# Seven-product gate-up units that overlap by one product, T1 in a tile of its own, and other places for the modulation products

## The chip, the cores and the metric

The kernel runs on one core of a Trainium2 chip. The metric is the device time of one execution in microseconds (us); the kernel before took 1917.07 us, the median of 3 runs (1916.01 to 1919.67).

## The reference, cut to what matters

A two-layer encoder trunk on x of 512 tokens by 1024 features in float32, conditioned by one vector c. Each layer has two SwiGLU feed-forward networks (FFNs) with a mixer between them:

```
cond = silu(c);  m = cond @ w_mod[l] + b_mod[l]        # shift, scale and gate of three sublayers, 9 x 1024
x = x + 0.5 * m[0,2] * swiglu(adaln(x, m[0]), w1, w3, w2)     # D_FF = 2752
x = x + m[1,2] * (mixer(adaln(x, m[1]) @ w_in) @ w_out)       # layer 0: windowed attention with a relative
x = x + 0.5 * m[2,2] * swiglu(adaln(x, m[2]), w1, w3, w2)     #   bias, short convolution; layer 1: dense
swiglu(h) = (silu(h @ w1) * (h @ w3)) @ w2                    #   attention, Hyena (a small MLP makes its filter)
adaln(x, m) = rmsnorm(x) * g * (1 + m[1]) + m[0]
```

## The kernel before, in words

Features stand on the partitions: x is 8 tiles of 128 features x 512 tokens. A float32 product is three matmuls: each operand is split into a rounded high part (ScalarE, L203) and the rest as a low part (VectorE, L204), and hi x hi, hi x lo and lo x hi are added up in PSUM. Weights are loaded to a `raw` tile of 512 KB (four of them in turn, on SyncE's DMA queue) and split to `wh` and `wl`.

Each of the four FFNs (layer l, place i = 0 or 2) has 21 gate-up units of 128 features (f = 0 to 20) and one of 64 (f = 21), in three groups: f = 0 to 4 and 21, 5 to 12, and 13 to 20. A group is its units and then a *down projection* (`project`, matmuls L358), which in 8 steps `dt` adds the group's part to x (L362). A *plain* unit is 48 matmuls of 512 columns and a glu (`glu`, L513 to L519). A *seven-product* unit (`up_seven`, L465) is Strassen-like: over blocks of 512 features x 256 tokens it needs seven products instead of eight, A11·B11, A12·B21, S2·T2, S1·T1, S3·T3, A22·T4 and S4·B22, each 12 matmuls of 256 columns (L477). S1 to S4 are sums of weight blocks, made on VectorE (`weight_sums`, L454 to L459) and split; T1 to T4 are sums of token blocks of h, made once for an FFN (`token_sums`, L398: h is computed again by L409 and L412, the sums are L418 to L421). T1 is written over the second half of h, so its split has to wait until the plain units have read that. A unit ends with copies and sums of the products (u1 L486, p + u1 L488, u2 L490, c22 L493, c22 + r L494, r + u2 L497), silu (L498), two multiplications (L499, L500) and a split to `ga`, `gb` or `gc`. PSUM has three banks "A", one "V" and two each of "Q" and "C"; A22·T4 goes to the bank that the copy of c22 empties.

The modulation vector m is computed column by column (`gemv`): a load of 512 KB of w_mod (L240) and one multiply-and-sum on VectorE (L248). These products are spread over the program: `rate` (in `ffn`) says how many go with each step of a group's down projection, by (l, i).

The order on each engine comes from a scheduler that moves instructions between the calls; an engine then works strictly down its list, and waits on semaphores. The relative bias (`rel_bias`, matmul L1099) and the Hyena filter (`hyena_filter`) are called between a group's units and its down projection.

## Time and profile before

| what | value |
|---|---|
| median of 3 runs | 1917.07 us |
| the profiled execution's own time; its span | 1918.76 us; 1917.0 us |
| busy: TensorE, VectorE, ScalarE | 1845.9, 1565.1, 1012.5 us |
| mean granted clock of TensorE | 0.988 of full speed |
| bytes from HBM | 258.88 MB |

The profile is one execution. A busy share is a mean over stages with different limits: of a stage one asks which wait ends last there. "PE" is TensorE's matmuls, "PEld" its weight loads, DVE VectorE, ACT ScalarE. A row `A <- B` means that A waited and B ended the wait. `PEclk` is the granted clock of TensorE as a share of full speed (1.00 is 2.4 GHz, 0.50 is 1.2 GHz).

### The profile page before, as it was taken

What the parts mean: (1) busy time and instruction counts of PE and PEld (TensorE: products, weight loads), DVE (VectorE), ACT (ScalarE), POOL (GpSimd) and SP (SyncE); (2) the same over time, 40 slices, a digit from 0 to 9 for tenths busy, and PEclk for the clock granted to TensorE, in tenths of its full rate; (3) what the DMA queues carried; (4) which work ended last, traced back from release to release, by engine and by line L of the source; (5) the groups of instructions that cost most, each with busy time, mean ns of one, the idle gap of its engine ahead of it and who ended that gap; (6) DMA issues with size and microseconds to landing.
All of it is one profiled execution on the core that took longest, in us unless ns stands there. A gap on an engine that the chain in (4) does not pass through costs nothing.

```text
span 1917.0 us, 30306 instructions
## 1 busy us (share of the span) xinstructions
PE 1845.9 (96%) x11844; PEld 1645.8 (86%) x11844; DVE 1565.1 (82%) x2681; ACT 1012.5 (53%) x1651; POOL 3.6 (0%) x9
## 2 busy tenths in 40 slices
PE   7889999999999999999989999998999999999999
PEld 5659889888888899798988989977887898898997
DVE  8989878878759898888899976877887889686682
ACT  5525435378848345254663533555788366353451
POOL 0000000000000000000000000000000000000000
PEclk9989999999999999999999999998999999999999
DMA  7664643842321644636427362344222322333231
GB/s 273 221 229 167 221 145 102 294 132 94 100 85 64 229 148 152 222 99 220 155 95 242 110 220 66 115 135 148 72 88 99 121 89 75 102 104 117 88 119 59
DMA packets 83658, 269.27 MB, mean 140 GB/s; under 512 B 10024, under 2 KB 13352, under 8 KB 83514
## 3 DMA queue, kind: packets, MB, share of 16 engines
q1 hardware_dynamic: 81898, 263.13, 41.0%
q0 software_dynamic: 1616, 4.20, 0.6%
q8 instruction: 93, 1.52, 0.3%
q14 instruction: 51, 0.42, 0.1%
HBM read 258.88 MB, written 10.50 MB: 141 GB/s over the span
## 4 chain that ended last, share of the span: by engine, by line
PE 73%; DVE 16%; DMA 6%; ACT 3%; issue 1%; SPq 0%; ACTq 0%; DVEq 0%
PE pA L477 29%; PE pC L358 18%; PE pV L477 5%; DVE wl L204 3%; PE pA L358 3%; DMA raw<-w2b 3%; DVE raw L248 2%; PE pC L225 2%; PE pC L226 2%; PE pC L224 2%; ACT wh L203 2%; DMA raw<-w2a 1%; DMA raw<-w_mod 1%; PE pA L789 1%; DVE h L345 1%
## 5 line engine op out<-in xcount | busy, mean ns | idle before, releaser
L203 ACT CAST wh<-raw 128x1024 fp32r<-128x1024 f32 (+2 forms) x393 | 372.8, 951 | 547.4 <-PE pA L477 194.6
L204 DVE TENSOR_TENSOR wl<-raw,wh 128x1024 fp32r<-128x1024 f32 (+2 forms) x393 | 432.1, 1102 | 120.3 <-ACT wh L203 117.1
L477 PE MATMUL pA<-h,wh 128*128 128x256 f32 x1752 | 331.2, 283 | 10.1 <-ACT h L203 9.2
L477 PE MATMUL pA<-e,wh 128*128 128x256 f32 x1752 | 333.4, 288 | 6.8 <-ACT tl L486 3.5
L477 PEld LDWEIGHTS pA<-e,wh 128*128 128x128 f32 x1752 | 271.5, 191 | 22.4 <-ACT tq L493 13.1
L477 PEld LDWEIGHTS pA<-h,wh 128*128 128x128 f32 x1752 | 275.7, 191 | 13.3 <-ACT h L203 9.9
L477 PE MATMUL pA<-e,wl 128*128 128x256 f32 x876 | 246.8, 282 | 0.0
L477 PE MATMUL pA<-h,wl 128*128 128x256 f32 x876 | 244.7, 283 | 1.9 <-DVE wl L204 1.9
L358 PE MATMUL pC<-gb,wh 128*128 128x512 f32 (+1 forms) x800 | 227.3, 368 | 3.6 <-ACT gb L203 1.6
L358 PE MATMUL pC<-ga,wh 128*128 128x512 f32 (+1 forms) x648 | 183.6, 371 | 5.0 <-DVE mod L261 2.6
L248 DVE SCALAR_TENSOR_TENSOR raw<-raw,cond 128x1024 f32<-128x1024 f32 x144 | 174.5, 1221 | 15.8 <-DMA raw<-w_mod 14.8
L358 PEld LDWEIGHTS pC<-gb,wh 128*128 128x128 f32 x800 | 143.9, 189 | 34.8 <-ACT gb L203 3.0
L477 PEld LDWEIGHTS pA<-h,wl 128*128 128x128 f32 x876 | 165.6, 189 | 2.3 <-DVE wl L204 2.3
L477 PEld LDWEIGHTS pA<-e,wl 128*128 128x128 f32 x876 | 167.4, 191 | 0.0
L358 PE MATMUL pC<-gb,wl 128*128 128x512 f32 (+1 forms) x392 | 143.8, 367 | 0.0
L358 PEld LDWEIGHTS pC<-ga,wh 128*128 128x128 f32 x648 | 115.5, 189 | 27.7 <-issue 3.9
L362 DVE SCALAR_TENSOR_TENSOR x<-pC,mod,x 128x512 f32<-128x512 f32 (+1 forms) x108 | 74.2, 687 | 74.7 <-PE pC L358 74.3
L358 PE MATMUL pC<-ga,wl 128*128 128x512 f32 (+1 forms) x300 | 111.6, 372 | 5.2 <-DVE wl L204 5.1
L203 ACT CAST wh<-e 128x1024 fp32r<-128x1024 f32 x73 | 76.8, 1052 | 60.6 <-PE pV L477 26.5
L477 PE MATMUL pV<-h,wh 128*128 128x256 f32 x584 | 107.1, 282 | 0.0
L225 PE MATMUL pA<-h,wh 128*128 128x256 f32 (+1 forms) x301 | 90.7, 310 | 2.1 <-DVE h L345 2.1
L477 PEld LDWEIGHTS pV<-h,wh 128*128 128x128 f32 x584 | 90.3, 190 | 0.0
(309 smaller groups left out, 3608.3 us busy)
## 6 DMA issues: line engine op xcount, KB each, us to landing
raw<-w SPq DMA_DIRECT2D x164, 512.0 KB, 3.5
raw<-w_mod SPq DMA_DIRECT2D x144, 512.0 KB, 4.5
raw<-w2b SPq DMA_DIRECT2D x64, 512.0 KB, 4.1
raw<-w_in SPq DMA_DIRECT2D x36, 512.0 KB, 4.5
raw<-w2a SPq DMA_DIRECT2D x32, 384.0 KB, 3.6
raw<-w_out SPq DMA_DIRECT2D x16, 512.0 KB, 3.4
raw<-w_start SPq DMA_DIRECT2D x8, 512.0 KB, 4.7
xs<-x SPq DMA_DIRECT2D x16, 256.0 KB, 2.0
```

The costliest lines, as they stand in the source:

```text
L203: self.nc.scalar.copy(out=hi, in_=src)
L204: self.nc.vector.tensor_sub(out=lo, in0=src, in1=hi.bitcast(F32))
L224: mm(out, lhsT=wh, rhs=rh, start=start, stop=False)
L225: mm(out, lhsT=wh, rhs=rl, start=False, stop=False)
L226: mm(out, lhsT=wl, rhs=rh, start=False, stop=stop)
L248: nc.vector.scalar_tensor_tensor(out=raw, in0=raw, scalar=1.0, in1=self.cond, op0=ALU.mult, op1=ALU.mult, accum_out=m[:, c : c + 1])
L345: nc.vector.tensor_sub(out=lo[:, c0:c1], in0=hf, in1=hi[:, c0:c1].bitcast(F32))
L358: nc.tensor.matmul(ps, lhsT=lh, rhs=r, start=q == 0, stop=q == len(todo) - 1)
L362: nc.vector.scalar_tensor_tensor(out=x, in0=ps, scalar=gate[dt], in1=x, op0=ALU.mult, op1=ALU.add)
L477: nc.tensor.matmul(out, lhsT=lh, rhs=rr, start=first and n == 0, stop=n == 11, skip_group_check=True)
L789: nc.tensor.transpose(tp[:, c * P : (c + 1) * P], pt[qb][:, o : o + P], self.ident)
```

## The change

`up_seven` of a unit now starts with its own A11·B11, then calls the rest of the unit before it (`finish`: A22·T4, the last product, silu, multiplications, split), and goes on with its own A12, S2, S1 and S3. Signs of the sums change so that the multiplications take a factor of -1 (`scalar_tensor_tensor`). Two weight sums stand ahead of the first split. The last unit of a group is finished in two halves. `token_sums` gets h as hi + lo; T1 stays in an `e3` tile and `first_sum` splits it into h after the plain units; the first seven-product unit of an FFN (`late_t1`) takes the product with T1 last. In the first FFN the units 5 to 7 are plain, and the token sums stand at f = 5. `rate` loses one product a step in the first down projection of the first three FFNs; `in_up` puts one product with each unit of some groups: 24 units in all. The relative bias moves from the first FFN's second to its third group. The three small layers of the Hyena filter (`filter_mlp`) move to the third FFN's second group.

```diff
-    def token_sums(self, key):
-
+    def token_sums(self):
 
         nc = self.nc
         t23, t4 = [], []
+        self.t1 = self.t("e3", (P, 1024))
...
-                a, b = self.ab[key + (kt,)]
-                xr = self.t("tq")
-                for c0, r in zip((0, HALF), self.rs):
-                    nc.vector.tensor_mul(
-                        out=xr[:, c0 : c0 + HALF], in0=self.x[kt][:, c0 : c0 + HALF], in1=r)
+                hi, lo = self.h[kt]
                 hf = self.t("th")
-                nc.scalar.activation(out=hf, in_=xr, func=AF.Identity, scale=a, bias=b)
+                nc.vector.tensor_add(out=hf, in0=hi.bitcast(F32), in1=lo.bitcast(F32))
...
-            s14, s23 = self.t("tq"), self.t("tq")
-            s1, s4, s2, s3 = s14[:, :HALF], s14[:, HALF:], s23[:, :HALF], s23[:, HALF:]
-            nc.vector.tensor_sub(out=s1, in0=b12, in1=b11)
-            nc.vector.tensor_sub(out=s2, in0=b22, in1=s1)
+            s4, s23 = self.t("tq")[:, :HALF], self.t("tq")
+            s1, s2, s3 = self.t1[:, j * HALF : (j + 1) * HALF], s23[:, :HALF], s23[:, HALF:]
+            nc.vector.tensor_sub(out=s1, in0=b11, in1=b12)
+            nc.vector.scalar_tensor_tensor(
+                out=s2, in0=s1, scalar=-1.0, in1=b22, op0=ALU.mult, op1=ALU.subtract)
             nc.vector.tensor_sub(out=s3, in0=b22, in1=b12)
-            nc.vector.tensor_sub(out=s4, in0=b21, in1=s2)
+            nc.vector.scalar_tensor_tensor(
+                out=s4, in0=s2, scalar=-1.0, in1=b21, op0=ALU.mult, op1=ALU.subtract)
...
-            self.split(s1, self.h[j][0][:, HALF:], self.h[j][1][:, HALF:])
...
+    def first_sum(self):
+
+        for j in range(4):
+            self.split(
+                self.t1[:, j * HALF : (j + 1) * HALF], self.h[j][0][:, HALF:], self.h[j][1][:, HALF:])
...
+        nc.vector.tensor_add(out=s[:, :T], in0=raw3[:, :T], in1=raw3[:, T:])
+        nc.vector.tensor_add(out=a21, in0=a21, in1=a11)
         x1 = self.split_new(raw1)
-        nc.vector.tensor_add(out=s[:, :T], in0=a21, in1=a22)
-        nc.vector.tensor_sub(out=s[:, T:], in0=s[:, :T], in1=a11)
+        cut = lambda pair, o: [v[:, o : o + T] for v in pair]
+        w = {"A11": cut(x1, 0), "A12": cut(x1, T)}
+        yield w
+        nc.vector.tensor_add(out=s[:, T:], in0=s[:, :T], in1=a11)
         x3 = self.split_new(s)
-        nc.vector.tensor_sub(out=a21, in0=a11, in1=a21)
         x2 = self.split_new(raw3)
-        nc.vector.tensor_sub(out=a12, in0=a12, in1=s[:, T:])
+        nc.vector.tensor_add(out=a12, in0=a12, in1=s[:, T:])
         x4 = self.split_new(a12)
-        cut = lambda pair, o: [v[:, o : o + T] for v in pair]
-        return {"A11": cut(x1, 0), "A12": cut(x1, T), "S1": cut(x3, 0), "S2": cut(x3, T), "S3": cut(x2, 0),
-                "A22": cut(x2, T), "S4": x4}
-
-    def up_seven(self, src1, src3, gh, gl):
-
-        nc = self.nc
-        w = self.weight_sums(src1, src3)
-        q, p, r = self.ps("A")[:, :HALF], self.ps("V")[:, :HALF], self.ps("A")[:, :HALF]
-
-        def product(out, a, b, first):
-            n = 0
-            for j in range(4):
-                wh, wl = (v[:, j * P : (j + 1) * P] for v in w[a])
-                rh, rl = self.rhs7[b][j]
-                for lh, rr in ((wh, rh), (wh, rl), (wl, rh)):
-                    nc.tensor.matmul(
-                        out, lhsT=lh, rhs=rr, start=first and n == 0, stop=n == 11, skip_group_check=True)
-                    n += 1
-
+        w.update({"S1": cut(x3, 0), "S2": cut(x3, T), "S3": cut(x2, 0), "A22": cut(x2, T), "S4": x4})
...
+    def up_seven(self, src1, src3, gh, gl, before, late_t1=False, halves=False):
...
+        sums = self.weight_sums(src1, src3)
+        w = next(sums)
+        q, p = self.ps("A")[:, :HALF], self.ps("V")[:, :HALF]
...
+        self.product(q, w["A11"], "B11", True)
         nc.scalar.copy(out=u1, in_=q)
-        product(p, "A12", "B21", True)
+        if before:
+            before()
+        next(sums, None)
+        r = self.ps("A")[:, :HALF]
+        self.product(p, w["A12"], "B21", True)
         nc.vector.tensor_add(out=sg[:, :HALF], in0=p, in1=u1)
-        product(q, "S2", "T2", False)
+        self.product(q, w["S2"], "T2", False)
         nc.scalar.copy(out=u2, in_=q)
-        product(r, "S1", "T1", True)
-        product(q, "S3", "T3", False)
+        if late_t1:
+            self.product(r, w["S4"], "B22", True)
+        else:
+            self.product(r, w["S1"], "T1", True)
+        self.product(q, w["S3"], "T3", False)
         nc.scalar.copy(out=c22, in_=q)
-        nc.vector.tensor_add(out=c22, in0=r, in1=c22)
-        product(q, "A22", "T4", False)
-        product(r, "S4", "B22", False)
-        nc.vector.tensor_add(out=sg[:, HALF:], in0=r, in1=u2)
-        nc.scalar.activation(out=sg, in_=sg, func=AF.Silu)
-        nc.vector.tensor_mul(out=sg[:, :HALF], in0=sg[:, :HALF], in1=q)
-        nc.vector.tensor_mul(out=sg[:, HALF:], in0=sg[:, HALF:], in1=c22)
-        self.split(sg, gh, gl)
+        nc.vector.tensor_tensor(out=c22, in0=c22, in1=r, op=ALU.subtract if late_t1 else ALU.add)
+
+        def finish():
+            self.product(q, w["A22"], "T4", False)
+            if late_t1:
+                self.product(r, w["S1"], "T1", False)
+                nc.vector.tensor_add(out=c22, in0=c22, in1=r)
+            else:
+                self.product(r, w["S4"], "B22", False)
+            neg = dict(scalar=-1.0, op0=ALU.mult, op1=ALU.mult)
+            if halves:
+                a, b = sg[:, :HALF], sg[:, HALF:]
+                nc.scalar.activation(out=a, in_=a, func=AF.Silu)
+                nc.vector.scalar_tensor_tensor(out=a, in0=q, in1=a, **neg)
+                self.split(a, gh[:, :HALF], gl[:, :HALF])
+                nc.vector.tensor_add(out=b, in0=r, in1=u2)
+                nc.scalar.activation(out=b, in_=b, func=AF.Silu)
+                nc.vector.scalar_tensor_tensor(out=b, in0=c22, in1=b, **neg)
+                self.split(b, gh[:, HALF:], gl[:, HALF:])
+                return
+            nc.vector.tensor_add(out=sg[:, HALF:], in0=r, in1=u2)
+            nc.scalar.activation(out=sg, in_=sg, func=AF.Silu)
+            nc.vector.scalar_tensor_tensor(out=sg[:, :HALF], in0=q, in1=sg[:, :HALF], **neg)
+            nc.vector.scalar_tensor_tensor(out=sg[:, HALF:], in0=c22, in1=sg[:, HALF:], **neg)
+            self.split(sg, gh, gl)
+
+        return finish
...
-        rate = {(0, 0): (2, 2, 2), (0, 2): (2, 2, 2), (1, 0): (2, 1, 0), (1, 2): (0, 0, 0)}[l, i]
+        rate = {(0, 0): (1, 2, 2), (0, 2): (1, 2, 2), (1, 0): (1, 1, 0), (1, 2): (0, 0, 0)}[l, i]
+        in_up = {(0, 0): (2,), (1, 0): (1, 2)}.get((l, i), ())
...
+            pending = None
             for f in fs:
                 gt[f] = new_g()
+                if g in in_up:
+                    self.gemv(1)
...
-                        self.token_sums((l, i))
-                elif first and g == 0:
+                        self.token_sums()
+                        self.first_sum()
+                elif first and (g == 0 or f < 8):
                     ps = self.up_banks()
                     for s in range(2):
                         w = self.weight(self.up_unit(k, 2 * f + s))
                         for kt in range(KT):
                             self.mm3(ps[s], self.block(w, kt), self.h[kt], kt == 0, kt == KT - 1)
-                        self.gemv(4)
+                        if g == 0:
...
+                            self.gemv(4)
                     self.glu(ps[0], ps[1], P, *gt[f])
-                    self.token_sums((l, i))
+                    if f == 5:
+                        self.token_sums()
+                    if f == 7:
+                        self.first_sum()
                 else:
-                    self.up_seven(self.up_unit(k, 2 * f), self.up_unit(k, 2 * f + 1), *gt[f])
-            if (l, i, g) == (0, 0, 1):
+                    pending = self.up_seven(
+                        self.up_unit(k, 2 * f), self.up_unit(k, 2 * f + 1), *gt[f], pending,
+                        late_t1=f == (8 if first else 2), halves=f == fs[-1])
+            if pending:
+                pending()
+            if (l, i, g) == (0, 0, 2):
                 self.rel_bias()
+            if (l, i, g) == (1, 0, 1):
+                self.filter_mlp()
             if (l, i, g) == (1, 0, 2):
                 self.hyena_filter()
...
-    def hyena_filter(self):
+    def filter_mlp(self):
...
-        w4 = self.t("raw", (P, 1024))[:64]
...
+        self.fsrc = src
+
+    def hyena_filter(self):
+
+        nc, ap = self.nc, self.ap
+        src = self.fsrc
+        w4 = self.t("raw", (P, 1024))[:64]
+        nc.sync.dma_start(out=w4, in_=ap["f_w4"])
```

On TensorE, in the second group of the last FFN: `pA_17379` holds S3·T3 and then A22·T4 of a unit, `pA_17507` A11·B11 of the next unit. Before:

```order
L477 MATMUL pA_17379<-e_2998_16752,wl_17371 128x256
L477 MATMUL pA_17507<-h_16274,wh_17487 128x256
L477 MATMUL pA_17507<-h_16275,wh_17487 128x256
L477 MATMUL pA_17507<-h_16274,wl_17488 128x256
L477 MATMUL pA_17507<-h_16276,wh_17487 128x256
L477 MATMUL pA_17379<-e_2972_16680,wh_17370 128x256
L477 MATMUL pA_17379<-e_2973_16681,wh_17370 128x256
L477 MATMUL pA_17379<-e_2972_16680,wl_17371 128x256
```

After, with `pA_17225` and `pA_17353` in these roles; the first two matmuls of A11·B11 stand ahead of the piece, behind S3·T3:

```order
L476 MATMUL pA_17353<-h_16055,wl_17350 128x256
L476 MATMUL pA_17353<-h_16057,wh_17349 128x256
L476 MATMUL pA_17353<-h_16058,wh_17349 128x256
L476 MATMUL pA_17353<-h_16057,wl_17350 128x256
L476 MATMUL pA_17353<-h_16059,wh_17349 128x256
L476 MATMUL pA_17353<-h_16060,wh_17349 128x256
L476 MATMUL pA_17353<-h_16059,wl_17350 128x256
L476 MATMUL pA_17353<-h_16061,wh_17349 128x256
L476 MATMUL pA_17353<-h_16062,wh_17349 128x256
L476 MATMUL pA_17353<-h_16061,wl_17350 128x256
L476 MATMUL pA_17225<-e_2926_16456,wh_17278 128x256
L476 MATMUL pA_17225<-e_2927_16457,wh_17278 128x256
```

Before, four matmuls of the next unit stood between S3·T3 and A22·T4; now all twelve do.

On VectorE, in the first down projection: L248 is a modulation product, L204 a split of weights, L362 the update of x. Before:

```order
L248 SCALAR_TENSOR_TENSOR raw_930,mod_1_0_864<-raw_930,cond 128x1024
L204 TENSOR_TENSOR wl_935<-raw_933,wh_934 128x768
L248 SCALAR_TENSOR_TENSOR raw_959,mod_1_0_864<-raw_959,cond 128x1024
L362 SCALAR_TENSOR_TENSOR x_68<-pC_908,mod_0_16_676,x_68 128x512
L625 CAST wh_934<-wl_935 64x128
L248 SCALAR_TENSOR_TENSOR raw_962,mod_1_0_864<-raw_962,cond 128x1024
L204 TENSOR_TENSOR wl_967<-raw_965,wh_966 128x768
L362 SCALAR_TENSOR_TENSOR x_69<-pC_940,mod_0_16_676,x_69 128x512
L625 CAST wh_966<-wl_967 64x128
L248 SCALAR_TENSOR_TENSOR raw_991,mod_1_0_864<-raw_991,cond 128x1024
L248 SCALAR_TENSOR_TENSOR raw_994,mod_1_0_864<-raw_994,cond 128x1024
L204 TENSOR_TENSOR wl_999<-raw_997,wh_998 128x768
```

After:

```order
L248 SCALAR_TENSOR_TENSOR raw_850,mod_1_0_764<-raw_850,cond 128x1024
L204 TENSOR_TENSOR wl_855<-raw_853,wh_854 128x768
L248 SCALAR_TENSOR_TENSOR raw_879,mod_1_0_764<-raw_879,cond 128x1024
L362 SCALAR_TENSOR_TENSOR x_67<-pC_773,mod_0_16_676,x_67 128x512
L672 CAST wh_854<-wl_855 64x128
L204 TENSOR_TENSOR wl_884<-raw_882,wh_883 128x768
L248 SCALAR_TENSOR_TENSOR raw_908,mod_1_0_764<-raw_908,cond 128x1024
L672 CAST wh_883<-wl_884 64x128
L204 TENSOR_TENSOR e_204_1050<-tq_1044,e_203_1049 128x512
L362 SCALAR_TENSOR_TENSOR x_68<-pC_802,mod_0_16_676,x_68 128x512
L204 TENSOR_TENSOR wl_913<-raw_911,wh_912 128x768
L248 SCALAR_TENSOR_TENSOR raw_937,mod_1_0_764<-raw_937,cond 128x1024
```

Two modulation products stood between two updates of x, and now one does; a split of a token sum (`e_204`) comes between.

On VectorE, at the start of the second FFN's seven-product units: `wl_6363` (before) and `wl_6149` (after) are the low part of A11 and A12 of the first of them, `e_` splits of token sums, `h_` splits of T1, L514 and L516 (L547, L549) the glu of plain units. Before:

```order
L204 TENSOR_TENSOR wl_6363<-raw_6357,wh_6362 128x1024
L457 TENSOR_TENSOR raw_6486<-raw_6485,raw_6486 128x512
L419 TENSOR_TENSOR tq_6292<-th_6289,tq_6291 128x256
L514 TENSOR_TENSOR tc_6210<-tc_6210,pA_5984 128x512
L420 TENSOR_TENSOR tq_6292<-th_6289,th_6284 128x256
L421 TENSOR_TENSOR tq_6291<-th_6289,tq_6292 128x256
L409 TENSOR_TENSOR tq_6305<-x_5449,rb_5745 128x256
L516 TENSOR_TENSOR ga_6209<-tc_6210,ga_6208 128x512
L204 TENSOR_TENSOR h_5870<-tq_6265,h_5869 128x256
L204 TENSOR_TENSOR e_1158_6298<-tq_6292,e_1157_6297 128x512
L204 TENSOR_TENSOR e_1150_6276<-tq_6291,e_1149_6275 128x256
L204 TENSOR_TENSOR h_5872<-tq_6291,h_5871 128x256
```

After:

```order
L414 SCALAR_TENSOR_TENSOR tq_6120<-e_1110_6062,th_6117 128x256
L204 TENSOR_TENSOR h_5677<-e_1110_6062,h_5676 128x256
L417 SCALAR_TENSOR_TENSOR tq_6119<-tq_6120,th_6117 128x256
L549 TENSOR_TENSOR ga_6023<-tc_6055,ga_6022 64x512
L204 TENSOR_TENSOR e_1138_6126<-tq_6120,e_1137_6125 128x512
L552 CAST ga_6023<-ga_6023 64x512
L204 TENSOR_TENSOR e_1132_6112<-tq_6119,e_1131_6111 128x256
L204 TENSOR_TENSOR h_5679<-e_1110_6062,h_5678 128x256
L204 TENSOR_TENSOR h_5681<-e_1110_6062,h_5680 128x256
L204 TENSOR_TENSOR h_5683<-e_1110_6062,h_5682 128x256
L456 TENSOR_TENSOR e_1143_6143<-raw_6142 128x512
L204 TENSOR_TENSOR wl_6149<-raw_6141,wh_6148 128x1024
```

The first unit's weights stood between the token sums of the first and the second block, and now stand behind all of these and behind the four splits of T1.

## Rows read from the trace of the kernel before

**Rows 1.** The page, busy us by engine (share of the span) x instructions.
```profile
PE 1845.9 (96%) x11844; PEld 1645.8 (86%) x11844; DVE 1565.1 (82%) x2681; ACT 1012.5 (53%) x1651; POOL 3.6 (0%) x9
```

**Rows 2.** Chain of waits, 1684 to 1706 us: start us, us, what x count.
```profile
1684.05 1.41 PE pV L477 x12
1685.46 8.74 PE pA L477 x72
```

**Rows 3.** Waits, weight loads (PEld) and matmuls (PE): us in total, times, longest.
```profile
PEld pA L477 <- ACT tq L493: 13.1, 66, 0.4
...
PE pA L477 <- ACT h L203: 9.2, 3, 3.1
PE pQ L992 <- DVE acc L978: 5.7, 1, 5.7
PE pC L358 <- ACT gc L203: 5.4, 5, 1.8
...
PE pA L477 <- ACT tl L486: 3.5, 2, 2.4
```

**Rows 4.** Windows, one unit: stretch, length, busy (x) by engine, PEclk, DMA share, GB/s.
```profile
1684.11:1694.26 10.15, 10.15 (x86) 9.96 (x85) 9.04 (x14) 5.79 (x10) 0.00 (x0) 1.00 0.31 102
```

**Rows 5.** Timeline, same unit: start, us, instruction, [idle before <-releaser].
```profile
1684.11 1.22 DVE L204 TENSOR_TENSOR wl<-raw,wh 128x1024 fp32r<-128x1024 f32 x1 [0.54 <-ACT wh L203]
...
1689.75 0.37 ACT L493 COPY tq<-pA 128x256 f32<-128x256 f32 x1 [0.48 <-PE pA L477]
```

**Rows 6.** The page, costliest groups: L204 and L248, busy, mean ns.
```profile
L204 DVE TENSOR_TENSOR wl<-raw,wh 128x1024 fp32r<-128x1024 f32 (+2 forms) x393 | 432.1, 1102 | 120.3 <-ACT wh L203 117.1
...
L248 DVE SCALAR_TENSOR_TENSOR raw<-raw,cond 128x1024 f32<-128x1024 f32 x144 | 174.5, 1221 | 15.8 <-DMA raw<-w_mod 14.8
```

**Rows 7.** Lines L362 and L499: count, ns min/median/max.
```profile
L362 DVE SCALAR_TENSOR_TENSOR x<-pA,mod,x x21: 385/484/752, 540.3 to 1561.2; 128x256 f32<-128x256 f32 x14, 128x512 f32<-128x512 f32 x7
...
L499 DVE TENSOR_TENSOR tc<-tc,pA x73: 404/414/423, 152.3 to 1871.7; 128x256 f32<-128x256 f32 x73
```

**Rows 8.** Windows, first down projection.
```profile
82.00:145.00 63.00, 47.12 (x198) 33.60 (x197) 56.99 (x107) 20.27 (x31) 1.24 (x1) 0.89 0.59 198
120.00:136.00 16.00, 13.45 (x54) 9.22 (x52) 13.07 (x24) 3.55 (x4) 0.00 (x0) 1.00 0.84 287
```

**Rows 9.** Chain of waits, first down projection.
```profile
87.74 0.60 DVE gb L516
...
132.17 3.76 PE pC L358 x15
```

**Rows 10.** The page, DMA issues: count, KB each, us to landing.
```profile
raw<-w_mod SPq DMA_DIRECT2D x144, 512.0 KB, 4.5
...
raw<-w2a SPq DMA_DIRECT2D x32, 384.0 KB, 3.6
```

**Rows 11.** Chain of waits, a down projection without stalls.
```profile
675.98 3.93 PE pC L358 x17
```

**Rows 12.** Chain of waits, start of the second FFN.
```profile
603.89 0.60 DVE tc L514
604.48 0.34 DVE tq L420
...
628.50 1.41 PE pV L477 x12
```

**Rows 13.** Timeline of TensorE, start of the second FFN.
```profile
609.11 0.40 PE L477 MATMUL pA<-h,wh 128*128 128x256 f32 x2
...
617.66 0.38 PE L477 MATMUL pA<-h,wh 128*128 128x256 f32 x1 [3.08 <-ACT h L203]
```

**Rows 14.** Windows around three stops of TensorE.
```profile
614.00:628.00 14.00, 9.98 (x55) 8.93 (x55) 12.69 (x24) 7.67 (x12) 0.00 (x0) 0.76 0.29 86
680.00:690.00 10.00, 7.56 (x52) 7.36 (x51) 9.93 (x15) 5.15 (x7) 0.00 (x0) 0.83 0.34 120
1290.00:1308.00 18.00, 11.62 (x57) 9.89 (x57) 13.99 (x26) 9.54 (x17) 0.00 (x0) 0.72 0.09 29
```

More of the change, by code (lines that the diff above doesn't have):

```diff
@@ L391, in project @@
         self.new_h()
-        self.rs = rs
         for c0, r in zip((0, HALF), rs):
@@ L448, in weight_sums @@
         raw1, raw3 = self.t("raw", (P, 1024)), self.t("raw", (P, 1024))
+        s = self.t("e3", (P, 1024))
+        a11, a12, a21 = raw1[:, :T], raw1[:, T:], raw3[:, :T]
         nc.sync.dma_start(out=raw1, in_=src1)
         nc.sync.dma_start(out=raw3, in_=src3)
-        s = self.t("e3", (P, 1024))
-        a11, a12, a21, a22 = raw1[:, :T], raw1[:, T:], raw3[:, :T], raw3[:, T:]
+        nc.vector.tensor_add(out=s[:, :T], in0=raw3[:, :T], in1=raw3[:, T:])
+        nc.vector.tensor_add(out=a21, in0=a21, in1=a11)
@@ new lines, in product @@
+    def product(self, out, w, b, first, last=False):
+        n = 0
+        for j in range(4):
+            wh, wl = (v[:, j * P : (j + 1) * P] for v in w)
+            rh, rl = self.rhs7[b][j]
+            for lh, rr in ((wh, rh), (wh, rl), (wl, rh)):
+                self.nc.tensor.matmul(
+                    out, lhsT=lh, rhs=rr, start=first and n == 0, stop=n == 11, skip_group_check=True)
+                n += 1
+    def up_seven(self, src1, src3, gh, gl, before, late_t1=False, halves=False):
+        nc = self.nc
+        sums = self.weight_sums(src1, src3)
+        w = next(sums)
+        q, p = self.ps("A")[:, :HALF], self.ps("V")[:, :HALF]
@@ L484, in up_seven @@
         sg = self.t("tc")
-        product(q, "A11", "B11", True)
+        self.product(q, w["A11"], "B11", True)
         nc.scalar.copy(out=u1, in_=q)
-        product(p, "A12", "B21", True)
+        if before:
[3 more added lines that the diff above has]
+        self.product(p, w["A12"], "B21", True)
         nc.vector.tensor_add(out=sg[:, :HALF], in0=p, in1=u1)
-        product(q, "S2", "T2", False)
+        self.product(q, w["S2"], "T2", False)
         nc.scalar.copy(out=u2, in_=q)
-        product(r, "S1", "T1", True)
@@ L548, in ffn @@
                             r = self.first_rstd()
-                            self.rs = [r[:, c0 : c0 + HALF] for c0 in (0, HALF)]
                             w = self.weight(self.ap["w13_start"][0])
@@ L918, in fold, with sin_tile @@
         nc.vector.tensor_sub(out=minus, in0=pe, in1=o)
-    def sin_tile(self, p, freq, freqb):
+    def sin_tile(self, p, freq, freqb, tag="tq"):
         nc = self.nc
-        a, k = self.t("tq")[:64], self.t("tq")[:64]
+        a, k = self.t(tag)[:64], self.t("tq")[:64]
         nc.scalar.activation(out=a, in_=p, func=AF.Identity, scale=freq, bias=freqb)
@@ L944, in hyena_filter @@
         nc.sync.dma_start(out=fc[:, :4], in_=ap["f_cols"])
-        nc.sync.dma_start(out=w4, in_=ap["f_w4"])
         for s in range(3):
@@ L951, in hyena_filter @@
             nc.tensor.matmul(p, lhsT=lw[s], rhs=src, start=True, stop=True)
-            src = self.sin_tile(p, fc[:, 3:4], fc[:, 4 + s : 5 + s])
+            src = self.sin_tile(p, fc[:, 3:4], fc[:, 4 + s : 5 + s], "tq" if s < 2 else "rb")
+        self.fsrc = src
[4 more added lines that the diff above has]
+        nc.sync.dma_start(out=w4, in_=ap["f_w4"])
         delta = self.t("rb")
```

## The prediction

> **What bounds the kernel now.** I read the page's busy times first: TensorE is busy for 1845.9 of 1917.0 us, VectorE for 1565.1, ScalarE for 1012.5 [rows 1]. So TensorE bounds the kernel, VectorE is the engine behind it, and a change can only gain by fewer or cheaper matmuls, or by filling the 71 us in which TensorE has no matmul and the stretches in which its clock is low. The chain of waits in a steady stretch of seven-product units shows how one unit costs 10.15 us: 12 matmuls in 1.41 and 72 in 8.74 [rows 2]. At 1.41 / 12 = 0.1175 us each, 84 matmuls would need 9.87 us; 0.28 us a unit is lost. The list of waits says where: the weight loads of L477 wait 66 times for the copy of c22 (L493), 13.1 us in all [rows 3]. In the windows view such a unit holds 9.04 us of VectorE work in 10.15 us, at clock 1.00 [rows 4]; the timeline shows the copy starting 0.48 us late, when the matmuls of S3 end, and VectorE's longest idle time of the unit, 0.54 us [rows 5]. The other losses are local: three waits for the split of T1, 9.2 us; one in the Hyena filter, 5.7 us; five for the last glu before a down projection, 5.4 us; two at the start of a group, 3.5 us [rows 3]. And there is one stretch where TensorE doesn't set the pace at all: from 82 to 145 us, the first down projection, it is busy for 47.12 of 63 us at a mean clock of 0.89 while VectorE is busy for 56.99 [rows 8].
>
> **Seven-product units that overlap.** The first order piece shows that four of the twelve A11 matmuls already stood ahead of A22. Now all twelve do, 1.41 us of cover for a copy whose wait is 0.28, so the wait goes. 73 such units ran before (the count of L499, [rows 7]); 70 remain. Of these, 24 now get a modulation product each (below). Of the other 46, eight are the last of their group, where no A11 follows; that leaves 38 x 0.28 = 10.6 us. TensorE's matmuls in a unit are the same in number.
> VectorE must fit under 9.87 us for that. Its list has the same 14 operations; two multiplications become scalar_tensor_tensor. The nearest rows are 484 ns for that form on a 128x256 PSUM tile against 414 for L499's multiplication [rows 7], so 9.04 + 2 x 0.07 = 9.18 us, 0.69 below the bound. The late idle of 0.54 us still fits (9.72). I take the full 10.6; if the slack were not enough, it would be nothing.
> The 24 units (third group of the first FFN, second and third of the third) are another matter: one modulation product costs 1.22 us on VectorE [rows 6], and 9.18 + 1.22 = 10.40 is above both 9.87 and 10.15. They become bound by VectorE: 24 x 0.25 = 6 us lost. Bounds: 24 x (9.87 - 10.15) = 6.7 us gained, if part of the list slides into idle time at the groups' ends, and with the 0.54 us wait left in, 10.94, 24 x 0.79 = 19 us lost. I take 6 lost.
>
> **The first down projection, fewer modulation products, three plain units.** Before, each of its 8 steps carried two modulation products (second order piece): two loads of 512 KB beside 384 KB of weights [rows 10], 1408 KB at the 287 GB/s of this stretch, which is 4.9 us, with DMA busy at 0.84 [rows 8], and the token sums and the relative bias besides. TensorE's own work for a step is 17 matmuls in 3.93 us [rows 11]. After, a step loads 896 KB, some 3.1 us at that rate, and VectorE has in it at most 1.10 (weights' low half), 1.22 [rows 6] and 0.75 (update, the longest in rows 7), 3.1 us: TensorE becomes the bound at 3.93 us. I let it start where the last gate-up value of the group came ready before, at 87.74 + 0.60 = 88.3 [rows 9], because the modulation products ahead of it in VectorE's order stay. Then 88 + 8 x 3.93 = 119.4 us instead of the 135.9 at which the last step ended (132.17 + 3.76) [rows 9]: 16.5 us gained. Paid back: the units 5 to 7 become plain, 48 matmuls of 512 columns at 3.93 / 17 = 0.231 us = 11.1 us instead of 10.15, 3 us in all. The token sums on VectorE lie beside their matmuls. Net 13.5 us gained. Bounds: 4 (if the loads still set the pace in half of the steps) to 19 (if the step starts 5 us earlier as well).
> The same at the start of the next groups: the first weights of the second FFN's second group come late, behind modulation products of the down projection; the two waits for the copy of u1 are 3.5 us [rows 3], and the clock in the 10 us from 680 on is 0.83 [rows 14], another 1.7. With one product a step instead of two both go: 5 us gained, bounds 0 and 7.
>
> **T1 in a tile of its own.** Three FFNs begin with token sums. Before, TensorE reached the first seven-product unit at 609.11, did 48 matmuls and stopped for 3.08 us at 617.66 for the split of T1 [rows 13]; the clock of 614 to 628 was 0.76 [rows 14]. The A12 product of the next unit began at 628.50 [rows 12]. What stands ahead of the unit's first weights in VectorE's order is what decides, and the third order piece shows that this got longer: wl of the first unit now stands behind all token sums and the four splits of T1. From the glu operation of the second plain unit on (L514 at 603.89 [rows 12], L547 after, itself counted) 25 VectorE instructions stand ahead of it; at 0.34 us from start to start for 256 and 0.60 for 512 columns [rows 12], and some 0.07 more for the scalar_tensor_tensor ones, these are 11.6 us, and wl itself 1.10 [rows 6]: ready at 616.6. So TensorE stands still from 609.1 to about 616.6, then has 96 matmuls (11.3 us), 1 to 1.5 us of waits for the next weights, and a low clock for some of it: 629 to 633 us for what ended at 628.50. The removed wait comes back, somewhat larger, ahead of the first product. I take 2 us lost each, 6 in all; bounds 9 us gained (the waits of rows 3 gone, nothing in their place) and 13 lost.
>
> **Tails and the Hyena filter.** The first step of a down projection waited for the last unit's output in five groups, 5.4 us by the row for gc alone [rows 3]. Now the last unit comes in halves, and 21 matmuls of the projection, 4.9 us, stand ahead of that wait in the last FFN, where 17 stood. Some of the five may be weights that land late instead, so I take 4 gained, bounds 0 and 6. The filter's small layers move to an earlier group; the wait for acc (5.7 us, [rows 3]) and the clock of 0.72 in the 18 us around it [rows 14], 5 us, have other causes beside these layers. I take 5 of 10.7; bounds 0 and 10.
>
> **Sum.** -10.6 + 6 - 13.5 - 5 + 6 - 4 - 5 = -26.1 us. The profiled execution took 1918.8 us, 1.8 beyond its span and 1.7 above the median of the three runs, 1917.1. From the median: 1891 us.
>
> **Rivals.** *VectorE becomes the bound of every seven-product unit (slower).* The margin of 0.69 us is in-order time: the sums of the next unit now stand early in VectorE's list and can wait for their weights while the multiplications behind them are due. For it: 9.18 of 9.87 us, and 82% busy overall [rows 1]. Against it: its longest idle time in a unit is 0.54 us. If all 70 units ran at 10.60 us, the gain of 10.6 would become a loss of 70 x 0.45 = 31.5 in place of the 6: -26.1 + 10.6 - 6 + 31.5 = +10, 1927 us. The break-even is a period of 10.46 us; from about 10.51 the kernel is measurably slower.
> *The clock pays for the longer stops.* TensorE standing still 7.5 us at three FFN starts, and near 88 us, could leave it at 1.2 GHz for longer than the 6 us lost hold: at 617 us 3.08 us of waiting were followed by 14 us at 0.76 [rows 13, 14], so a further 14 x 0.24 = 3.4 us each, 10 in all: 1901 us. For the stop itself the third order piece speaks; against the price, that the granted clock was low there before, too. [...]
> *The first down projection stays bound by loads and VectorE.* With only 4 of its 13.5 us gained: 1900 us. For it: DMA at 0.84 busy. Against: 36% fewer bytes.
> *The T1 and product terms cost nothing.* The two losses of 6 us are absorbed, VectorE's idle times at the ends of groups taking up the one, and the other not arising because the first unit's weights are split sooner than I count: 1879 us.
> *Nothing remains.* The two costs at their bounds (19 and 13 lost) and the first down projection at 4: 1917.1 + (-10.6 + 19 - 4 - 5 + 13 - 4 - 5) = 1920.5 us.
>
> **Chances.** The forecast (1891, its own range 1883 to 1898) 0.47; absorbed losses 0.16; clock 0.13; first down 0.12; nothing remains 0.05; VectorE everywhere 0.07. 0.2% is 3.8 us, about what a measurement of this kernel can tell from no change. Faster by more than that: all of the first four and the lower part of the fifth, 0.90; within it the rest of the fifth and a little of the last, 0.04; slower 0.06. The range 1870 to 1907 leaves out the last two cases and the far ends of the others.
>
> **What will show it.** Right: the wait for c22 gone from the list, units of 84 matmuls each 9.87 us in the last FFN; units of 10.4 us with VectorE without idle time in the third FFN; in the first down projection updates of x 3.9 us apart, the last near 119 us; TensorE idle for 7 us at about the start of the first unit in three FFNs, waiting for wl or h. Wrong: units above 10.15 us where no modulation product runs, or updates in the first down projection still 5 us apart.

## The result, and the profile after

The changed kernel takes 1896.3 us (median of 4 runs, 1892.0 to 1898.7); its ratio to the kernel before is 0.9891, with a 95% interval from 0.9867 to 0.9915. Measured again beside later experiments: 1894.6 us, ratio 0.9877 (0.9857 to 0.9896). That is 21 to 24 us faster; 26 were forecast. The profiled execution took 1898.7 us, with a span of 1896.9. A second one was profiled with the later measurement (span 1892.8); single stages of the two differ by up to 4 us, and where that matters both are given.

Busy times after, which answer to [rows 1]:

```profile
PE 1831.8 (97%) x11736; PEld 1642.3 (87%) x11736; DVE 1547.3 (82%) x2634; ACT 987.9 (52%) x1625; POOL 3.6 (0%) x9
```

TensorE is busy for 14 us less and idle for 6 us less; matmul stalls of some tenths and slow matmuls count as busy here (a unit of 10.15 us was busy for all of it, [rows 4]), and the mean clock is 0.986, where it was 0.988. The waits of weight loads for the copy of c22, which answer to the first line of [rows 3]:

```profile
PEld pA L476 <- ACT tq L507: 3.4, 11, 0.9
```

13.1 us in 66 waits have become 3.4 in 11. The longest waits of matmuls after:

```profile
PE pA L476 <- DVE wl L204: 19.2, 3, 6.9
PE pC L358 <- DVE x L362: 7.4, 3, 4.2
```

The first is new: two waits of 6.9 us and one of 5.3 at the starts of FFNs, in the place of the three for T1's split. The second stands in third down projections, twice in the first FFN (2.2 and 4.2 us) and once in the second. In the last FFN the unit's period can be read on VectorE, from one unit's first multiplication to the next one's:

```profile
1699.07 0.42 DVE L530 SCALAR_TENSOR_TENSOR tc<-pA,tc 128x256 f32<-128x256 f32 x1
...
1708.96 0.42 DVE L530 SCALAR_TENSOR_TENSOR tc<-pA,tc 128x256 f32<-128x256 f32 x1
```

9.89 us, where it was 10.15 [rows 4]. These rows also show the form that I priced 0.07 us above a plain multiplication: 0.42 us, as before.

Windows after, each for a stage with its own story: the first down projection and what follows it ([rows 8] before), the start of the second FFN ([rows 14]), the third down projection of the first FFN, the first mixer, and the end of the third FFN with the Hyena filter:

```profile
82.00:145.00 63.00, 59.98 (x247) 47.94 (x246) 53.38 (x91) 21.05 (x28) 0.00 (x0) 0.95 0.56 183
605.00:620.00 15.00, 8.06 (x46) 7.74 (x45) 14.91 (x27) 7.15 (x12) 0.00 (x0) 0.66 0.08 24
335.00:390.00 55.00, 48.52 (x290) 43.31 (x289) 40.73 (x72) 20.87 (x34) 1.24 (x1) 0.94 0.78 276
390.00:531.00 141.00, 137.55 (x731) 113.34 (x730) 113.08 (x242) 106.73 (x231) 0.00 (x0) 1.00 0.32 105
1254.00:1316.00 62.00, 61.98 (x396) 53.34 (x396) 46.98 (x78) 35.12 (x57) 0.00 (x0) 1.00 0.39 136
```

And the last three stages before:

```profile
348.60:397.30 48.70, 45.87 (x290) 40.55 (x289) 39.95 (x71) 21.06 (x34) 0.00 (x0) 1.00 0.77 262
397.30:534.30 137.00, 136.21 (x731) 112.84 (x729) 113.50 (x243) 109.72 (x234) 0.00 (x0) 1.00 0.34 107
1253.00:1334.00 81.00, 72.94 (x416) 59.89 (x416) 61.12 (x106) 42.38 (x67) 0.00 (x0) 0.94 0.32 111
```

The stage with the filter runs at a clock of 1.00, where it was 0.94. Its two windows do not begin at the same matmul; from the last matmul of the third FFN's units to the last one of the down projection it is 81.7 us before and 66.2 after, so 15.5 us shorter. Before:

```profile
1251.92 0.28 PE L477 MATMUL pA<-h,wl 128*128 128x256 f32 x1
...
1333.64 0.28 PE L358 MATMUL pC<-gc,wl 128*128 128x256 f32 x1
```

After:

```profile
1250.20 0.28 PE L476 MATMUL pA<-h,wl 128*128 128x256 f32 x1
...
1316.37 0.28 PE L358 MATMUL pC<-gc,wl 128*128 128x256 f32 x1
```

The third down projection went from 48.7 to 55 us and the mixer from 137 to 141: there the change lost what nothing in my sum spoke of. The lead over the kernel before, read at the last matmul of some stages, shows how the gain comes about:

| up to the end of | first profile, us ahead | second profile, us ahead |
|---|---|---|
| the units of the first FFN's second group | 14.7 | 16.8 |
| the first FFN's third down projection | 7.1 | 8.2 |
| the second FFN | 3.5 | 7.4 |
| the units of the third FFN's third group | 1.7 | 5.4 |
| the Hyena filter and the down projection beside it | 17.3 | 20.9 |
| the kernel | 20.1 | 24.2 |

The lead of the first FFN is mostly lost again, and the stage with the filter brings the larger part of the net gain. Of the low point, 2 to 4 us are the filter's small layers, which the change has done by then: the second down projection of the third FFN, which now holds them, is that much longer than before.

### The profile page after: what moved, and what is told of

It is laid out like the page before. It is cut to its first block, busy times and chain, and to the rows that moved or that the text cites. A ratio compares the mean times of both kernels' runs of the same rounds, so it can differ in the third digit from the quotient of the medians.

```text
span 1896.9 us, 29947 instructions
## 1 busy us (share of the span) xinstructions
PE 1831.8 (97%) x11736; PEld 1642.3 (87%) x11736; DVE 1547.3 (82%) x2634; ACT 987.9 (52%) x1625; POOL 3.6 (0%) x9
## 4 chain that ended last, share of the span: by engine, by line
PE 79%; DVE 12%; DMA 5%; ACT 2%; issue 1%; SPq 0%; ACTq 0%; DVEq 0%
PE pA L476 26%; PE pC L358 20%; PE pV L476 4%; PE pA L358 4%; DVE wl L204 3%; DMA raw<-w2b 3%; PE pC L225 2%; PE pC L224 2%; PE pC L226 2%; DVE raw L248 2%; PE pA L225 2%; PE pA L226 2%; PE pA L224 2%; DMA raw<-w_mod 1%; ACT wh L203 1%
## 5 line engine op out<-in xcount | busy, mean ns | idle before, releaser
L203 ACT CAST wh<-raw 128x1024 fp32r<-128x1024 f32 (+2 forms) x390 | 371.6, 954 | 484.4 <-PE pA L476 137.1
L204 DVE TENSOR_TENSOR wl<-raw,wh 128x1024 fp32r<-128x1024 f32 (+2 forms) x390 | 429.7, 1104 | 97.1 <-ACT wh L203 92.2
L476 PE MATMUL pA<-e,wh 128*128 128x256 f32 x1680 | 309.2, 282 | 2.6 <-ACT tl L501 2.5
L476 PE MATMUL pA<-h,wh 128*128 128x256 f32 x1680 | 309.1, 282 | 0.4 <-DVE tc L528 0.4
L476 PEld LDWEIGHTS pA<-e,wh 128*128 128x128 f32 x1680 | 257.6, 189 | 7.3 <-ACT tl L501 3.8
L476 PEld LDWEIGHTS pA<-h,wh 128*128 128x128 f32 x1680 | 259.9, 191 | 1.7 <-DVE tc L528 0.6
L476 PE MATMUL pA<-h,wl 128*128 128x256 f32 x840 | 238.2, 284 | 19.2 <-DVE wl L204 19.2
L476 PE MATMUL pA<-e,wl 128*128 128x256 f32 x840 | 234.9, 280 | 0.0
L248 DVE SCALAR_TENSOR_TENSOR raw<-raw,cond 128x1024 f32<-128x1024 f32 x144 | 174.9, 1220 | 17.3 <-DMA raw<-w_mod 16.6
L476 PEld LDWEIGHTS pA<-h,wl 128*128 128x128 f32 x840 | 159.3, 190 | 19.8 <-DVE wl L204 19.8
L476 PEld LDWEIGHTS pA<-e,wl 128*128 128x128 f32 x840 | 158.4, 189 | 0.0
L362 DVE SCALAR_TENSOR_TENSOR x<-pC,mod,x 128x512 f32<-128x512 f32 (+1 forms) x108 | 74.1, 686 | 74.5 <-PE pC L358 74.3
L225 PE MATMUL pA<-h,wh 128*128 128x256 f32 (+1 forms) x333 | 102.9, 316 | 1.2 <-DVE h L345 1.2
L226 PE MATMUL pA<-h,wl 128*128 128x256 f32 (+1 forms) x333 | 102.7, 313 | 0.0
```

What stands on the lines that cost most here:

```text
L203: self.nc.scalar.copy(out=hi, in_=src)
L204: self.nc.vector.tensor_sub(out=lo, in0=src, in1=hi.bitcast(F32))
L225: mm(out, lhsT=wh, rhs=rl, start=False, stop=False)
L226: mm(out, lhsT=wl, rhs=rh, start=False, stop=stop)
L248: nc.vector.scalar_tensor_tensor(out=raw, in0=raw, scalar=1.0, in1=self.cond, op0=ALU.mult, op1=ALU.mult, accum_out=m[:, c : c + 1])
L362: nc.vector.scalar_tensor_tensor(out=x, in0=ps, scalar=gate[dt], in1=x, op0=ALU.mult, op1=ALU.add)
```

## The experiments

All but one start from the changed kernel. A ratio is to the kernel before, timed in the same set of runs.

**The overlap.** The next unit begins only after `finish`:

```
-                        late_t1=..., halves=f == fs[-1])
+                        late_t1=..., halves=f == fs[-1])
+                    pending()
+                    pending = None
```

> Changed kernel, but each seven-product unit is finished before the next begins in program order (the scheduler may still move matmuls). Theory: the overlap of one product is what took away the wait for the copy of c22; without it 38 units cost 0.28 us more, units of 10.15 us in the last FFN instead of 9.87, about 1896 + 10 = 1906 us. Rival: the gain in these units is from the new order of the weight sums, and the scheduler pulls A11 ahead anyway: 1896 to 1899 us and units of 9.9 us.

1901.0 us, ratio 0.9918 (0.9893 to 0.9942), between the theory's 1906 and the rival's 1899. The wait for the copy of c22 is back, and a unit of the last FFN takes 10.16 us again (1676.85 - 1666.69):

```profile
PEld pA L476 <- ACT tq L507: 12.9, 64, 0.8
```

```profile
1666.69 0.42 DVE L530 SCALAR_TENSOR_TENSOR tc<-pA,tc 128x256 f32<-128x256 f32 x1
...
1676.85 0.42 DVE L530 SCALAR_TENSOR_TENSOR tc<-pA,tc 128x256 f32<-128x256 f32 x1
```

So the theory holds in the rows: 9.5 us more of that wait. By the ratios the kernel is 5 to 8 us slower, with intervals that leave room for 10.

**The modulation products where they were before.**

```
-        rate = {(0, 0): (1, 2, 2), (0, 2): (1, 2, 2), (1, 0): (1, 1, 0), ...
-        in_up = {(0, 0): (2,), (1, 0): (1, 2)}.get((l, i), ())
+        rate = {(0, 0): (2, 2, 2), (0, 2): (2, 2, 2), (1, 0): (2, 1, 0), ...
+        in_up = ()
```

> Changed kernel with the modulation products where they were before: two a step in the first down projections of the first three FFNs, none with the units. Theory: the first down projection was bound by the loads of these products, so its steps go back from about 4.3 to about 5 us, 6 to 10 us more there, 5 us more at the start of the second FFN's second group, and 2 to 4 us less in the groups whose units lose their product: 1904 to 1908 us. Rival: what slowed that projection were the token sums and the relative bias, which stay away: its steps stay near 4.3 us and the time at 1893 to 1898 us.

1893.2 us, ratio 0.9884 (0.9853 to 0.9914): the rival's time, though the edit also takes the products out of the units, so that the time alone does not part the two. In the first down projection the updates of x, here the first and the seventh, come as early as in the changed kernel. Changed kernel:

```profile
93.35 0.75 DVE L362 SCALAR_TENSOR_TENSOR x<-pC,mod,x 128x512 f32<-128x512 f32 x1
...
118.93 0.75 DVE L362 SCALAR_TENSOR_TENSOR x<-pC,mod,x 128x512 f32<-128x512 f32 x1
```

With two products a step:

```profile
92.22 0.75 DVE L362 SCALAR_TENSOR_TENSOR x<-pC,mod,x 128x512 f32<-128x512 f32 x1 [0.16 <-PE pC L358]
...
116.24 0.75 DVE L362 SCALAR_TENSOR_TENSOR x<-pC,mod,x 128x512 f32<-128x512 f32 x1
```

**Where the relative bias stands.** In the changed kernel the relative bias's transfer of 2 MB, issued by GpSimd at 337.6 us, runs beside the weight loads of the third down projection. The edit calls it in the loop over units, behind unit 8:

```
+                if (l, i, f) == (0, 0, 8):
+                    self.rel_bias()
...
-            if (l, i, g) == (0, 0, 2):
-                self.rel_bias()
```

> Changed kernel with the relative bias called after the first seven-product unit (f = 8) of the first FFN, so that its transfer of 2 MB runs beside seven-product units. Theory: in the changed kernel this transfer lies in the third down projection of the first FFN, whose loads land later for it (55.2 us instead of 48.7): 6 us less there and perhaps 1 to 3 in the mixer behind it, 1887 to 1890 us. Rival: that projection is slower because of the modulation products' own loads behind units that now also load them: no change, 1894 to 1898 us.

1886.5 us, ratio 0.9842 (0.9819 to 0.9866). GpSimd's issue of the transfer in the changed kernel, and here:

```profile
337.58 1.24 POOL L1158 DMA_DIRECT2D vec<-vec  x1 [337.13 <-DMA vec<-th]
```

```profile
164.69 1.24 POOL L1158 DMA_DIRECT2D vec<-vec  x1 [164.25 <-DMA vec<-th]
```

And the third down projection and the mixer here:

```profile
334.30:386.20 51.90, 47.10 (x290) 42.16 (x289) 40.73 (x72) 20.95 (x34) 0.00 (x0) 0.97 0.75 253
386.20:523.30 137.10, 136.32 (x730) 112.97 (x729) 113.51 (x243) 109.65 (x234) 0.00 (x0) 1.00 0.34 107
```

Some 3 us come back in the projection, and all 4 in the mixer. Before, the transfer was issued at 141 us, among the units. The projection's own weights (`w2b`) land later beside it. Time from issue to landing in us (the last figure), changed kernel from 330 to 392 us, and this one from 326 to 388:

```profile
raw<-w2b SPq DMA_DIRECT2D x5, 512.0 KB, 7.9
```

```profile
raw<-w2b SPq DMA_DIRECT2D x6, 512.0 KB, 4.8
```

The other 3 us of the projection's 6.5 stay when the transfer has gone.

**The filter's layers called where they were.** `filter_mlp()` directly ahead of `hyena_filter()`:

> Changed kernel with the three small layers of the Hyena filter called right before the rest of the filter, as before, in the third FFN's third group. Theory: the stage from that group's down projection to the mixer, 80.7 us before and 62.2 after, is shorter by 18.5 us because these layers no longer stand in one chain with the rest of the filter: 1896 + 15 = 1911 us (14 to 19 more). Rival: the layers' own waits were 3 us and the rest of the 18.5 comes from elsewhere: 1897 to 1901 us.

1909.0 us, ratio 0.9955 (0.9939 to 0.9970): 12 to 15 us slower by the ratios, at the theory's lower end and far from the rival. The stage is as long as before, at as low a clock:

```profile
1240.00:1322.00 82.00, 72.10 (x410) 59.05 (x409) 60.16 (x104) 44.50 (x68) 0.00 (x0) 0.92 0.32 110
```

**What held the first down projection.** First, units 5 to 7 as seven-product units and the token sums behind unit 4, as before:

```
-                elif first and (g == 0 or f < 8):
+                elif first and g == 0:
...
-                    if f == 5:
+                    if f == 4:
                         self.token_sums()
-                    if f == 7:
                         self.first_sum()
...
-                        late_t1=f == (8 if first else 2), ...
+                        late_t1=f == (5 if first else 2), ...
```

> Changed kernel with units 5 to 7 of the first FFN as seven-product units again, and the token sums, the splits of T1 among them, called right behind unit 4, as before. Rates and relative bias stay as changed. Theory: the token sums on VectorE are what held the first down projection back, not the loads (with two products a step it ended as early as with one): its steps go back to 5 us or more, 8 to 12 us lost, 3 us of the plain units gained: 1901 to 1906 us. Rival: the matmul of the relative bias and its load did it, which stay away: the projection keeps its 37 us, and the time is 1892 to 1895 us.

1894.0 us, ratio 0.9875 (0.9858 to 0.9891), which meets the rival's number for another reason: the scheduler had pulled the relative bias forward into this projection.

```profile
PE pQ L1151 <- DMA th<-rel_hot: 8.2, 1, 8.2
```

The second down projection began 12 us late, at 217.3 us, and later stages gave it back, since the transfer no longer met the third: that projection and the mixer took 10 us less. So this run didn't tell the two apart. Two more do, with the product of the relative bias in a bank A, so that it can't move ahead of the units. In the kernel before:

> The kernel before, with one edit: the relative bias called behind unit 8 of the first FFN, its product in one of the banks A so that it stays among the units, and away from the first down projection. Theory: in that projection VectorE's token sums set the pace, and TensorE waiting 5.2 us for the relative bias's table cost next to nothing beside them: 1914 to 1917 us. Rival: TensorE's wait for this table and the low clock behind it were the loss there: 8 to 13 us gained, 1904 to 1909 us.

1917.3 us, ratio 0.9995 (0.9982 to 1.0007): no gain. The wait for the table is gone, and another stands in its place, for weights behind the token sums in VectorE's list:

```profile
PE pC L358 <- DVE wl L204: 11.0, 4, 9.8
```

And in the variant of the changed kernel:

> The kernel with units 5 to 7 of the first FFN as seven-product units and the token sums in the first down projection, now with the relative bias behind unit 8 as well, its product in one of the banks A. Theory: the token sums on VectorE cost the first down projection and the units behind it 8 to 12 us even without the relative bias: against the kernel with the relative bias moved alone (1886.5 us) 1894 to 1898 us, the second down projection of the first FFN starting at 213 to 217 us instead of 205. Rival: only the relative bias slowed that projection: 1882 to 1887 us, that start at 203 to 206 us.

1891.5 us, ratio 0.9861 (0.9844 to 0.9878); the second down projection begins at 209.8 us, between the two theories' figures (before: 220.2; with plain units 204.8). The wait is the same one:

```profile
PE pC L358 <- DVE wl L204: 11.4, 1, 11.4
```

The first projection itself takes 44.8 us from its first to its last matmul, where the kernel with the relative bias moved alone takes 35.8: the token sums in it cost 9 us. To take them out costs the 3.6 us of three plain units, so that the move is worth 5 us of that stretch. The other 10 us of the 15 come with cheaper sums, the overlap, one product a step and the relative bias's absence together, and I didn't part these; by `rates_back` one product a step isn't the main part.

**The halves.** `halves=False`:

> Changed kernel without the two halves in the last unit of a group. Theory: the halves bring nothing where a down projection has modulation products, since one of these stands between the halves on VectorE (at 648 us TensorE waits 2.4 us): 1894 to 1898 us, that wait back at about 1.2 us. Rival: the halves are worth the predicted 4 us: 1899 to 1902 us, waits for gc and gb longer in all groups.

1891.2 us, ratio 0.9866 (0.9849 to 0.9883): no slower than the changed kernel.

**T1's product in third place.** `late_t1=False`:

> Changed kernel in which the first seven-product unit of an FFN takes the product with T1 in third place, as all others do; T1 stays in its own tile. Theory: TensorE's wait at the start of that unit is for the low part of A11's weights behind all token sums on VectorE, 7 us, and the order of its products changes nothing in it: 1895 to 1898 us, the same three waits of about 7 us. Rival: the late product is what keeps a second wait, for T1's split, away: 2 to 3 us more in each of three FFNs, 1902 to 1906 us.

1893.3 us, ratio 0.9874 (0.9856 to 0.9893), with the same three waits, 19.2 us. The order of the products makes no measurable difference there.

**A plain unit for the token sums to stand beside.** On top of the moved relative bias:

```
-                    if not first:
-                        self.token_sums()
-                        self.first_sum()
-                elif first and (g == 0 or f < 8):
+                elif first and (g == 0 or f < 8) or f == 2:
...
-                    if f == 5:
+                    if f == (5 if first else 2):
                         self.token_sums()
-                    if f == 7:
+                    if f == (7 if first else 2):
                         self.first_sum()
...
-                        late_t1=f == (8 if first else 2), ...
+                        late_t1=f == (8 if first else 3), ...
```

> The kernel with the relative bias behind unit 8 (1886.5 us), and unit 2 of the other three FFNs a plain one, so that the token sums stand beside its 48 matmuls and its weights ahead of most of them on VectorE; the first seven-product unit is then unit 3. Theory: the three waits of 7 us for the weights and the low clock behind them, 8 to 10 us each, go, and each plain unit costs 1.2 us more than a seven-product one: 6 to 8 us gained in each, 1863 to 1869 us. Rival: VectorE's list is what bounds the start and has got two more splits: the wait only moves behind the plain unit, 1885 to 1890 us.

1863.4 us, ratio 0.9725 (0.9706 to 0.9743), 22 to 23 us below the kernel with the relative bias moved alone, and 29 to 33 below the changed one. The three waits for `wl` are gone from the list. 50 us at the start of the second FFN, in both from 59 us behind the end of the mixer, changed kernel and this one:

```profile
590.00:640.00 50.00, 43.06 (x323) 41.82 (x322) 47.73 (x88) 29.40 (x51) 0.00 (x0) 0.90 0.21 67
```

```profile
580.00:630.00 50.00, 49.06 (x333) 44.89 (x332) 48.88 (x90) 28.60 (x49) 0.00 (x0) 1.00 0.31 103
```

TensorE has 6 us more matmul time and its clock is 1.00 instead of 0.90; the mean over the kernel is 0.999.

**The same without the halves,** and **the changed kernel again:**

> The kernel with unit 2 plain and the relative bias moved (1863.4 us), without the two halves in the last unit of a group. Theory: the halves bring nothing, the modulation products on VectorE come between them: 1860 to 1865 us. Rival: the halves bring the predicted 4 us: 1866 to 1869 us.

1864.8 us, ratio 0.9723 (0.9703 to 0.9743): the halves bring nothing here either.

> The changed kernel itself, for a closer interval beside the others: every theory expects 1893 to 1898 us.

1894.6 us, as given above.

## Why the prediction was right, and where it wasn't

The direction and the size held: 21 to 24 us where 26 were forecast. But that the sum came out is in good part luck: several terms were off, and two large errors cancelled. Without the filter's move the kernel gains 6 to 12 us (`filter_back`), where the sum without that term was 21; the filter's move brought 7 to 10 us more than forecast, and the relative bias, which the sum left out, cost 7 to 9.

- *Overlap (-10.6).* Right: 9.9 us units, and 9.5 us of the wait return when it is undone.
- *24 units with a modulation product (+6).* In the third group of the first FFN eight units took 81.8 us before, 81.7 in the first profile of the changed kernel and 85.4 in the second; I took 2 more. In the other profiles with these products they took 83 to 86, without them (`rates_back`) 81.2. VectorE isn't busy throughout even in the longer one, 78.48 of 85.4 us.

```profile
248.00:333.40 85.40, 82.03 (x675) 79.95 (x674) 78.48 (x126) 46.04 (x71) 0.00 (x0) 1.00 0.48 159
```

  The other 16 units stand in the third FFN, and there the step failed: units of 10.40 us would be 83.2 us for eight, and the two groups take 81.5 each, less than before (83.2 and 81.7) and 1.4 us more than eight units without a product in the last FFN (80.1).

```profile
1040.18:1121.65 81.47, 81.04 (x677) 80.13 (x676) 75.33 (x120) 46.10 (x71) 0.00 (x0) 1.00 0.47 157
1168.93:1250.48 81.55, 80.83 (x676) 79.60 (x674) 70.65 (x114) 47.03 (x73) 2.13 (x4) 1.00 0.46 154
```

  The term was mis-sized: VectorE's list of one such unit, fifteen operations back to back, takes 10.07 us there, where I had 10.40, and that lies below the 10.15 of before.

```profile
1061.45 0.68 DVE L204 TENSOR_TENSOR wl<-raw,wh 128x512 fp32r<-128x512 f32 x1
...
1071.52 0.69 DVE L204 TENSOR_TENSOR wl<-raw,wh 128x512 fp32r<-128x512 f32 x1
```

  The 0.2 us above the 9.87 of the matmuls agree with the 1.4 us for eight units. Over all 24 the time is about as before, not 6 us more; what the 2 to 4 us in the first FFN come from isn't shown.
- *First down projection (-13.5).* The size was about right: with the units behind it, 137.1 us before (83.1 to 220.2) and 121.2 after (84.3 to 205.5), 15.9 us less, about 1.4 of it from the overlap in five units. The updates of x are 4.2 us apart on average, where 3.9 were forecast and 5.7 was the time before. The step "TensorE becomes the bound because a step loads 896 KB instead of 1408" failed: with 1408 KB the updates come as early. Shown in its place are the token sums in VectorE's list, with 9 us in the projection; the rest of what bounded it stays open.
- *Start of the second FFN's second group (-5).* Its units took 85.7 us and now take 80.7, of which the overlap is 2; with the old rate they take 82.1, so the rate isn't the main cause. Without the overlap they take 81.7, and no wait comes back there either. What the cause is stays open.
- *T1 (+6).* The mechanism was right: TensorE stops for `wl` behind the token sums and the splits of T1, and `wl` is ready 7.5 us after the units' start, as forecast.

```profile
613.13 0.58 PE L476 MATMUL pA<-h,wl 128*128 128x256 f32 x1 [6.93 <-DVE wl L204]
```

```profile
611.94 1.15 DVE wl L204
...
613.13 2.50 PE pA L476 x10
615.63 2.13 PE pV L476 x10
...
626.59 1.41 PE pV L476 x12
```

From 605.6 on it starts two matmuls each of A11 and A12, and then stops for 6.93 us; the A12 product of the next unit comes 21 us after the units' start, where it was 19.4 [rows 12, 13]. Over the three FFNs the first group's units took 116.3 us before (38.6, 39.8, 37.9) and 119.1 after: 3 us lost, not 6. Of the clock rival's 3.4 us at a start, about 15 x 0.34 - 14 x 0.24 = 1.7 us shows in the second FFN (0.66 for 15 us in the place of 0.76 for 14, [rows 14]), inside these 3. (In the second profile they took 3.9 us more than before, not 2.8.)
- *Tails (-4).* Wrong: the halves bring nothing measurable, in two pairs of kernels. In the third down projection of the first FFN, for example, VectorE does two modulation products between 336 and 339 us, inside the second half; that these are the reason isn't shown.
- *Hyena filter (-5).* Mis-sized: the stage became 15.5 us shorter, and undoing this edit alone costs 12 to 15 us. I had halved what the rows of the wait and the clock offered, 10.7 us; all of it was to be had and more: the wait for acc is gone, and the clock is 1.00.
- *Relative bias (not in the sum).* The change moves a transfer of 2 MB from among the units to a down projection that already loaded at 262 GB/s. Of the 6.5 us lost there some 3 are the transfer's, and all 4 in the mixer. The prediction named the relative bias only as a load on the first down projection and left out where its transfer goes; moving it again brought 7 to 9 us by the ratios.

## What to carry to other kernels

When a step moves, its transfers move with it: ask what else loads in the new place. An engine that works in order is best read as a list: what stands ahead of the first instruction that the bound engine needs decides, and the cheapest repair may be to put a slower but self-sufficient piece of work (here one plain unit, 1.2 us dearer) on the bound engine while that list runs. And a stage that has both a wait and a low clock may offer both: in the filter's stage and at the starts of the FFNs the clock went to 1.00 when the wait went.

## What the runs showed that I had not expected

A stop costs more than the wait's row tells: three waits of 19.2 us in all went, three units became 1.2 us dearer each, and 22 to 23 us were gained, 7 more than the 15.6 of the waits; the mean clock of the profiled executions rose from 0.989 to 0.999. The rows above show a price of this size: behind the stop at 606 us, 20 matmuls take 2.50 + 2.13 = 4.63 us, where 12 take 1.41 at full clock, so 20 take 2.35; that is 2.3 us lost at each of three starts if the other two are like this one. And a `scalar_tensor_tensor` with a constant took 0.42 us on a 128x256 tile, no more than a multiplication of two tensors, where the form with a column of scalars had 0.48 [rows 7]; what makes the difference wasn't tested.
